# Re-laying a gated attention and FFN block on eight cores: tokens by residue, attention first, a listed order per engine, resident FFN weights

## The chip, the cores and the metric

One Trainium2 chip, eight cores, one sequence of 2048 tokens on each; the cores exchange nothing. The time is that of the slowest core, in microseconds (us) on the device. A program on all eight cores has a second, slower state in some of its executions, in which the cores of one die show a lower granted TensorE clock. Engines: PE is TensorE, PEld its weight loads, DVE VectorE, ACT ScalarE, POOL GpSimd, SP SyncE (it only issues transfers here); a "q" after a name is the engine's sequencer.

## The reference, cut to what matters

```python
h = rms_norm(x, norm_mix_pre)                       # x: 2048 x 1024 per core
u_a, v_a, q, k, v_b, g_a, g_b = split(h @ w_in)     # seven blocks of 1024 columns
y_a = chunked_spatial_gating(gelu(u_a), gelu(v_a))  # branch A: layer norm of v, then tril(W_s) over chunks of 128
y_b = dilated_attention_mixture(q, k, v_b)          # branch B: 16 heads of 64, three patterns below
merged = sigmoid(g_a + b) * (y_a @ w_a_proj) + sigmoid(g_b + b) * (y_b @ w_b_proj)
x = x + rms_norm(merged @ w_out)
f = square(relu(rms_norm(x) @ w_ff1)) @ w_ff2       # 1024 -> 4096 -> 1024
x = x + rms_norm(f)
```

The attention runs every head under (window, dilation) = (128, 1), (512, 4) and (2048, 16), with ALiBi bias, and mixes the three by their softmax denominators. That mixture is the same as adding the three numerators, adding the three denominators, and dividing once.

## The kernel before

Stages run one after the other: norm and transposes, branch A, then attention head pair by head pair, gates, output projection and FFN. The parts that the change touches, with cuts marked:

```python
# operands of a score matmul: tokens in sequence order, so dilations 4 and 16 are steps in the access pattern
def tokapN(T, p, kb, nblk):
    if p == 0: return T[:, 128 * kb:128 * kb + 128 * nblk]
    if p == 1: ...; return T[:, s:s + 4 * (128 * nblk - 1) + 1:4]
    return T[:, kb:SEQ:16]
# Q of each head has 128 rows, of which the other head's 64 are zero:
S.op("dve", lambda e, i=i: e.memset(QZ[i][0][64:128, :], 0.0), ...)
mm(ps[bank][:, ...], tokap(KT[d], slice(0, 128), p, kb), tokapN(QZ[d][hh], p, kb, nblk), ...)
# values: 65 stationary columns (64 of V and one of ones); each dilation is closed in PSUM and added in fp32
mm(ps[bank][:65, acol:acol + n], vaug[d][:, 16 * p + vblk, hh, :], PT[...][:, ptcol:ptcol + n], i == 0, True, ...)
S.op("dve", lambda e: e.tensor_tensor(out=av, in0=ps[bank][0:65, :]..., in1=av, op=ALU.add), ...)
# ... V is transposed on TensorE 48 times per pair; denominators go through DRAM to be inverted and broadcast
S.barrier()                                       # after branch A, after attention, after the gates
for w in range(4):                                # FFN: both weights fetched again for each window
    S.dma("pool", ... out=w1b[b], in_=w1s_d[fq] ...)
    ...
    mm(ps[pk][:, :], w2b[b][:, fb, :], hid[:, fb, :], ...)          # output comes channel-major
    S.op("pe", lambda e, cb=cb: e.transpose(out=..., in_=fT[:, cb, 128 * ti:128 * ti + 128], identity=identf[:]), ...)
```

The softmax here doesn't subtract the row's maximum and nothing guards it: scores larger than these inputs give would overflow.

Of the kernel before, what the change touches and what calls it, by code (L numbers as in the profile page):

```python
# [8 lines left out]
F32 = mybir.dt.float32  # L9
# [6 lines left out]
NCORES = 8  # L16

class Sched:
    ENGS = ("pe", "act", "dve", "pool", "sp")

    def __init__(self, nc):
        self.nc = nc
        self.es = ExitStack()
        self.lists = {e: [] for e in self.ENGS}
        self.sem = {e: self.es.enter_context(nc.semaphore("s_" + e)) for e in self.ENGS}
        self.cnt = {e: 0 for e in self.ENGS}
        self.waited = {e: {} for e in self.ENGS}
        self.lastw = {}
        self.readers = {}
        self.dma_sems = {}  # L30
        self.dma_cnt = {}

    def _need(self, eng, dep):
        key, sem, val = dep
        if key == eng and eng == "pe":
            return
        w = self.waited[eng]
        if w.get(key, 0) >= val:
            return
        w[key] = val  # L40
        self.lists[eng].append(("wait", sem, val))

    def _deps(self, eng, reads, writes):
        for b in list(reads) + list(writes):
            d = self.lastw.get(b)
            if d is not None:
                self._need(eng, d)
        for b in writes:
            for d in self.readers.get(b, ()):
                self._need(eng, d)  # L50

    def _mark(self, tok, reads, writes):
        for b in writes:
            self.lastw[b] = tok
            self.readers[b] = []
        for b in reads:
            self.readers.setdefault(b, []).append(tok)

    def op(self, eng, fn, reads=(), writes=(), signal=True):
        self._deps(eng, reads, writes)  # L60
        if signal:
            self.cnt[eng] += 1
            self.lists[eng].append(("op", fn, self.sem[eng], 1))
            tok = (eng, self.sem[eng], self.cnt[eng])
        else:
            self.lists[eng].append(("op", fn, None, 0))
            tok = (eng, self.sem[eng], self.cnt[eng] + 1)
        self._mark(tok, reads, writes)

    def dma(self, queue, fn, chan, reads=(), writes=()):  # L70
        if chan not in self.dma_sems:
            self.dma_sems[chan] = self.es.enter_context(self.nc.semaphore("d_" + str(chan)))
            self.dma_cnt[chan] = 0
        self._deps(queue, reads, writes)
        self.dma_cnt[chan] += 16
        sem = self.dma_sems[chan]
        self.lists[queue].append(("op", fn, sem, 16))
        tok = ("dma_" + str(chan), sem, self.dma_cnt[chan])
        self._mark(tok, reads, writes)

    def barrier(self):
        toks = [(e, self.sem[e], self.cnt[e]) for e in ("pe", "act", "dve", "pool") if self.cnt[e] > 0]
        toks += [("dma_" + str(c), self.dma_sems[c], self.dma_cnt[c]) for c in self.dma_sems]
        for e in self.ENGS:
            for t in toks:
                if t[0] != e:
                    self._need(e, t)
                elif e != "pe":
                    self._need(e, t)

    def emit(self):
        nc = self.nc
        lists = self.lists

        def replay(lst, e):
            for it in lst:
                if it[0] == "wait":
                    e.wait_ge(it[1], it[2])
                else:
                    ins = it[1](e)  # L100
                    if it[2] is not None:
                        ins.then_inc(it[2], it[3])
# [21 lines left out]
        self.es.close()  # L124

def tokap(T, rows, p, blk):
    if p == 0:
        return T[rows, 128 * blk:128 * blk + 128]
    if p == 1:
        c, n = blk // 4, blk % 4  # L130
        s = 512 * n + c
        return T[rows, s:s + 509:4]
    return T[rows, blk:SEQ:16]

def build_nc():
# [6 lines left out]
    win_d = din("w_in", [56, 128, 1024])  # L142
    wa_d = din("w_a", [8, 128, 1024])
    wb_d = din("w_b", [8, 128, 1024])
    wo_d = din("w_o", [128, 8, 1024])
    w1_d = din("w_1", [128, 8, 4096])
    w2_d = din("w_2", [16, 128, 2048])
    wsT_d = din("wsT", [128, 8, 128])
    bs_d = din("b_s", [1, 1024])
    lgrow_d = din("ln_g_row", [1, 1024])  # L150
    lb_d = din("ln_b", [128, 8])
    bg_d = din("b_gate", [128, 16])
    gains_d = din("gains", [4, 1024])
    ident_d = din("ident", [128, 128], BF16)
    identf_d = din("identf", [128, 128])
    mask_d = din("mask", [128, 128])
    ones_d = din("onesf", [128, 128])
    eb_d = din("eb", [128, 80, 128], BF16)
    out_d = nc.dram_tensor("out", [SEQ, DM], F32, kind="ExternalOutput").ap()
    den_d = nc.dram_tensor("den_scr", [16, SEQ], F32).ap()  # L160
    w1s_d = nc.dram_tensor("w1_bf", [8, 128, 4096], BF16).ap()
    w2s_d = nc.dram_tensor("w2_bf", [8, 128, 4096], BF16).ap()

    S = Sched(nc)
    top = ExitStack()

    def sb(stack, name, shape, dt):
        return stack.enter_context(nc.sbuf_tensor("sb_" + name, list(shape), dt))
# [11 lines left out]
    ssq = stat[:, 0:16]  # L180
    rstd = stat[:, 16:32]
    varall = stat[:, 32:48]
    rstdv = stat[:, 48:64]

    cvn = [0]

# [684 lines left out]
```

## Time and profile before

| what | before |
|---|---|
| time, median of four runs beside the changed kernel | 1584.78 us |
| time, three runs | 1583.41 us |
| PE busy, share of the span | 84% |
| DMA moved per core | 165.70 MB |
| start to first score of attention | about 264 us |
| attention, eight pairs | 492.5 us |
| gates | 225.8 us |
| output projection and FFN | 572.7 us |

The prediction below shows the chain and the stretches. One more reading belongs here, three groups of the page's list of costliest groups (line, engine, operation, operands, shapes, count; busy us, mean ns of one; idle time before them and what ended it):

```profile
L518 ACT ACTIVATE sb_Et<-pst 128x512 bf16<-128x512 f32 x320 | 177.0, 567 | 98.2 <-PE pst L218 40.2
L553 DVE TENSOR_TENSOR sb_acc<-pst,sb_acc 65x512 f32<-65x512 f32 x64 | 69.2, 1081 | 0.1
L557 DVE TENSOR_TENSOR sb_acc<-pst,sb_acc 65x512 f32<-65x512 f32 x64 | 67.0, 1046 | 2.9 <-PE pst L218 0.5
```

The first line is the exponential, 512 columns at a time; the other two are the adds that put dilations 4 and 16 on top of dilation 1. They cost over 1 us each, but VectorE as a whole was not the bound. To compare kernels by stage I use five marks on TensorE's timeline: the first score matmul, the last value matmul, the first gate matmul, the first output projection, the end.

### The profile page before, as it was taken

The page shows a single profiled execution, that of the slowest core. Times are in us where ns is not written, and L with a number is a line of the kernel's source. Part 1 is how long each engine was busy: PE and PEld are TensorE (multiplying, and loading weights), DVE is VectorE, ACT ScalarE, POOL GpSimd, SP SyncE. Part 2 cuts the span into 40 slices and gives each one's busy share as a digit, 9 for nine tenths or more (in the row PEclk, how much of TensorE's full clock was granted, in tenths as well). Part 3 has the DMA queues.
Part 4 walks back from the last instruction along what each step waited for, and adds up shares of the span by engine and source line. Part 5 has one row for each costly group of instructions (what it writes and reads, how often), then busy time and mean ns, then how long its engine had stood idle before and what let it go on. Part 6 is the DMA issues. An engine that isn't in the chain of part 4 may idle for free.

```text
span 1588.4 us, 23161 instructions; the slowest of 8 cores (1567.5 to 1588.4 us)
## 1 busy us (share of the span) xinstructions
PE 1341.3 (84%) x7092; PEld 689.6 (43%) x7092; DVE 663.9 (42%) x1104; ACT 696.4 (44%) x1351; POOL 162.4 (10%) x206
## 2 busy tenths in 40 slices
PE   1498928897998898976199999869999999999994
PEld 1244514554555555543044444324444444444442
DVE  2675661565566555656122332333205404412402
ACT  2423306656756666664055555444314414513302
POOL 1100740001001000000111110000000000000000
PEclk9999959998998989976599999879999999999997
DMA  8830043265465364434574442224245543634532
GB/s 190 154 34 1 1 50 61 42 128 96 107 123 98 100 125 98 103 95 114 80 99 41 41 40 27 94 66 153 113 159 161 184 176 130 199 133 148 197 133 79
DMA packets 116487, 165.70 MB, mean 104 GB/s; under 512 B 79744, under 2 KB 90880, under 8 KB 108160
## 3 DMA queue, kind: packets, MB, share of 16 engines
q0 software_dynamic: 96928, 104.87, 31.8%
q1 hardware_dynamic: 19440, 59.37, 12.0%
q8 instruction: 60, 0.98, 0.2%
q14 instruction: 59, 0.48, 0.1%
HBM read 174.44 MB, written 25.43 MB: 126 GB/s over the span
## 4 chain that ended last, share of the span: by engine, by line
PE 67%; DMA 13%; DVE 8%; issue 5%; ACT 4%; SPq 1%; DVEq 0%; POOL 0%; ACTq 0%; POOLq 0%
PE pst L218 66%; DMA sb_wqkv<-w_in 5%; DMA sb_xt<-x 2%; DMA sb_denbc<-den_scr 2%; DMA sb_dsm<-den_scr 2%; DVE sb_acc L557 2%; DVE sb_bst L311 1%; DVE sb_big L314 1%; DVE sb_t L699 1%; DMA den_scr<-sb_acc 1%; DMA sb_wg<-w_in 1%; PE pst L746 1%; ACT sb_vaug L458 1%; ACT sb_Et L518 1%; ACT sb_gv L308 1%
## 5 line engine op out<-in xcount | busy, mean ns | idle before, releaser
L218 PE MATMUL pst<-sb_h2T,sb_big 128*128 128x512 bf16 x1024 | 228.5, 382 | 2.4 <-ACT sb_h2T L737 1.3
L218 PE MATMUL pst<-sb_hT,sb_w2b 128*128 128x512 bf16 x1024 | 223.6, 379 | 1.5 <-DVE sb_hT L778 1.5
L218 PE MATMUL pst<-sb_hT,sb_wqkv 128*128 128x512 bf16 x768 | 201.6, 412 | 25.2 <-DMA sb_wqkv<-w_in 24.8
L518 ACT ACTIVATE sb_Et<-pst 128x512 bf16<-128x512 f32 x320 | 177.0, 567 | 98.2 <-PE pst L218 40.2
L218 PEld LDWEIGHTS pst<-sb_h2T,sb_big 128*128 128x128 bf16 x1024 | 100.5, 98 | 123.6 <-issue 7.9
L218 PEld LDWEIGHTS pst<-sb_hT,sb_w2b 128*128 128x128 bf16 x1024 | 99.6, 98 | 119.8 <-issue 1.9
L218 PE MATMUL pst<-sb_PT,sb_vaug 128*65 128x128 bf16 (+1 forms) x816 | 112.1, 260 | 44.0 <-DVE sb_PT L534 11.6
L218 PE MATMUL pst<-sb_hT,sb_wg 128*128 128x512 bf16 x512 | 118.2, 385 | 33.5 <-DMA sb_wg<-w_b 33.5
L778 DVE TENSOR_TENSOR sb_hT<-sb_hT 128x512 bf16<-128x512 bf16 x128 | 50.2, 422 | 224.3 <-ACT sb_hT L776 224.1
L218 PEld LDWEIGHTS pst<-sb_hT,sb_wqkv 128*128 128x128 bf16 x768 | 81.1, 107 | 119.3 <-issue 50.5
L528 DVE TENSOR_TENSOR sb_PT<-sb_Et,sb_EBh 128x512 bf16<-128x512 bf16 x176 | 73.4, 425 | 140.4 <-ACT sb_Et L518 136.2
L218 PEld LDWEIGHTS pst<-sb_PT,sb_vaug 128*65 128x65 bf16 x816 | 82.7, 122 | 84.6 <-issue 60.3
L218 PE MATMUL pst<-sb_QZ_1,sb_KT 128*128 128x256 bf16 (+1 forms) x384 | 96.2, 355 | 21.2 <-ACT sb_Et L518 21.1
L776 ACT ACTIVATE sb_hT<-pst 128x512 bf16<-128x512 f32 x128 | 73.0, 595 | 85.2 <-PE pst L218 85.0
L218 PE MATMUL pst<-sb_QZ_0,sb_KT 128*128 128x256 bf16 (+1 forms) x384 | 98.6, 373 | 5.4 <-ACT sb_Et L518 4.1
L792 ACT ACTIVATE sb_yaT<-pst 128x512 f32<-128x512 f32 x32 | 19.1, 597 | 179.7 <-PE pst L218 179.6
L653 ACT ACTIVATE sb_sg<-pst,sb_bg 128x512 f32<-128x512 f32 x64 | 43.4, 678 | 114.2 <-PE pst L218 114.2
L218 PEld LDWEIGHTS pst<-sb_hT,sb_wg 128*128 128x128 bf16 x512 | 50.6, 99 | 95.7 <-issue 36.9
L660 DVE TENSOR_TENSOR sb_tA<-pst,sb_sg 128x512 f32<-128x512 f32 x32 | 22.1, 692 | 114.1 <-ACT sb_sg L656 107.3
L553 DVE TENSOR_TENSOR sb_acc<-pst,sb_acc 65x512 f32<-65x512 f32 x64 | 69.2, 1081 | 0.1
L557 DVE TENSOR_TENSOR sb_acc<-pst,sb_acc 65x512 f32<-65x512 f32 x64 | 67.0, 1046 | 2.9 <-PE pst L218 0.5
L218 PE MATMUL pst<-sb_wout,sb_merged 128*128 128x512 bf16 x256 | 61.1, 395 | 2.2 <-DVE sb_merged L664 2.2
(102 smaller groups left out, 1606.1 us busy)
## 6 DMA issues: line engine op xcount, KB each, us to landing
sb_big<-w_bf POOLq DMA_DIRECT2D x32, 1024.0 KB, 6.3
sb_w2b<-w_bf POOLq DMA_DIRECT2D x32, 1024.0 KB, 5.2
sb_stg<-w POOLq DMA_DIRECT2D x32, 512.0 KB, 5.6
w_bf<-sb_stg SPq DMA_DIRECT2D x32, 512.0 KB, 3.9
sb_xt<-x SPq DMA_DIRECT2D x16, 512.0 KB, 5.3
sb_denbc<-den_scr SPq DMA_DIRECT2D x32, 256.0 KB
sb_xo<-x SPq DMA_DIRECT2D x16, 512.0 KB, 5.3
out<-sb_xo SPq DMA_DIRECT2D x16, 512.0 KB, 2.8
```

The lines of the kernel that those rows point to most:

```text
L218: S.op("pe", lambda e: e.matmul(out, lhsT=lhsT, rhs=rhs, start=start, stop=stop, skip_group_check=True), reads=reads, writes=writes, signa ...
L308: S.op("act", lambda e, hf=hf, pk=pk: e.activation(out=gv[:, 512 * hf:512 * hf + 512], in_=ps[pk + hf][:, :], func=AF.Gelu_apprx_tanh), re ...
L311: S.op("dve", lambda e, hf=hf: e.bn_stats(out=bst[:, 6 * hf:6 * hf + 6], in_=gv[:, 512 * hf:512 * hf + 512]), reads=[f"gv{hf}"], writes=[" ...
L518: S.op("act", lambda e: e.activation(out=Et[es][:, 0:W], in_=ps[bank][:, 0:W], func=AF.Exp), reads=[], writes=[PK[bank], f"Et{es}"])
L528: S.op("dve", lambda e: e.tensor_tensor(out=PT[ptb][:, :].rearrange("p (a q) -> p a q", q=256), in0=Et[es][:, :].rearrange("p (a q) -> p a ...
L553: S.op("dve", lambda e: e.tensor_tensor(out=av, in0=ps[bank][0:65, :].rearrange("p (n i) -> p n i", n=4), in1=av, op=ALU.add), reads=[], w ...
L557: S.op("dve", lambda e: e.tensor_tensor(out=av, in0=ps[bank][0:65, :].rearrange("p (r i) -> p r i", r=4), in1=av, op=ALU.add), reads=[], w ...
L653: S.op("act", lambda e, j=j, cb=cb, po=po: e.activation(out=sg[j][:], in_=ps[po + j][:, :], func=AF.Exp, scale=-1.0, bias=bg[:, 8 * j + cb ...
L660: S.op("dve", lambda e, po=po: e.tensor_tensor(out=tA[:], in0=ps[po + 2][:, :], in1=sg[0][:], op=ALU.mult), reads=["sg0"], writes=[PK[po + ...
L776: S.op("act", lambda e, fb=fb, pk=pk: e.activation(out=hid[:, fb, :], in_=ps[pk][:, :], func=AF.Relu), reads=[], writes=[PK[pk], f"hid{fb}"])
L778: S.op("dve", lambda e, fb=fb: e.tensor_tensor(out=hid[:, fb, :], in0=hid[:, fb, :], in1=hid[:, fb, :], op=ALU.mult), reads=[], writes=[f" ...
L792: S.op("act", lambda e, cb=cb, pk=pk: e.activation(out=fT[:, cb, :], in_=ps[pk][:, :], func=AF.Copy), reads=[], writes=[PK[pk], f"fT{cb}"])
```

## The change: its intent, and the diff

The kernel is written anew. Tokens are stored by residue modulo 16, so that a dilated read is a run of neighbours. Attention comes first, so that branch A's weights arrive behind it. The two heads of a pair use rows 0 to 63 and 64 to 127 of TensorE, and the values of all three dilations add up in one PSUM bank per head. V is made token-major and put into the other two orders by a trip through DRAM. The FFN's weights are converted to bfloat16 in DRAM during attention and loaded once. FFN 2 writes tokens by rows, so that its output needs no transposes. A small scheduler decides the order on each engine beforehand, from assumed durations. The core of it:

```diff
-                    mm(ps[bank][:, ...], tokap(KT[d], slice(0, 128), p, kb), tokapN(QZ[d][hh], p, kb, nblk), ...)
+                rows = slice(64 * hh, 64 * hh + 64)
+                kv, qv = view(KT[d], rows), view(QT[d], rows)
+                ...
+                else:
+                    kk = kv[:, blk, :]
+                    qq = qv[:, blk, :]
+                mms.append((psall[:, sb + hh, n0:n0 + nn], kk, qq, n == 0, n == len(blocks) - 1, nn, False))
-                    S.op("dve", lambda e: e.tensor_tensor(out=av, in0=ps[bank][0:65, :]..., in1=av, op=ALU.add), ...)
+        for j in range(8):            # dilation 1: first matmul of a bank sets, the others add
+            ... mms.append((out(hh, 0, 4, 8 * blk, w), lhs(V0[d], blk, hh), ..., first[hh], False, 4 * w, False))
+        for n2 in range(2):           # dilation 4 adds
+        for a in range(4):            # dilation 16 adds and closes
+            mms.append((ps(bks[hh])[:, 128 * a:128 * a + 128], stg[sd][...], p2t[...], False, a == 3, 128, False))
+    def load_v(hp, prio):             # 32 transfers out of DRAM per head pair, on SyncE's queue
+        ... fns.append(lambda e, ...: e.dma_start(out=V1[d][32 * a:32 * a + 32, 4 * c:4 * c + 4, :], in_=...))
+        ... fns.append(lambda e, b=b: e.dma_start(out=V0[d][:, b, :], in_=s0[b][:, :, 192 * hh:192 * hh + 192]))
+        its.append(... e.dma_start(out=w1s_d[f], in_=w1_d[f]) ...)   # fp32 to bfloat16, DRAM to DRAM, 24 of them
+            P.pe([(ps(bb[hf]), hid[:, fb, 128 * ti:128 * ti + 128], w2[:, fb, 512 * hf:512 * hf + 512], ...)
+                  for fb in range(32)], ...)                         # FFN 2, tokens by rows
+    def dma(self, q, fns, nbytes, chan, ...):
+        o = self._add(q, list(fns), cost, reads, writes, prio, nb=nbytes, chan=chan, lat=2.0, name=name)
```

The last two lines belong to the scheduler: every transfer is taken to land 2 us after its bytes have passed.

## The prediction

> **What bounds the kernel now.** I read the chain that ended last first. It is TensorE for two thirds, transfers for an eighth, and little else:
>
> ```profile
> PE 67%; DMA 13%; DVE 8%; issue 5%; ACT 4%; SPq 1%; DVEq 0%; POOL 0%; ACTq 0%; POOLq 0%
> ```
>
> So I looked for the stages (TensorE's timeline shows where the operands change) and asked for busy time in each stretch. Columns: stretch, its length, busy us and instructions of PE, PEld, DVE, ACT, POOL, then granted clock, DMA share and GB/s.
>
> ```profile
> 0.00:74.50 74.50, 19.76 (x133) 13.74 (x134) 32.23 (x37) 25.72 (x65) 9.98 (x15) 1.00 0.88 180
> 74.50:135.50 61.00, 56.72 (x257) 24.42 (x256) 42.94 (x75) 16.50 (x30) 4.38 (x5) 1.00 0.27 27
> 135.50:212.00 76.50, 64.21 (x385) 32.72 (x383) 47.25 (x58) 23.93 (x40) 40.76 (x31) 0.95 0.00 1
> 212.00:232.70 20.70, 0.02 (x1) 0.06 (x2) 14.36 (x6) 0.00 (x0) 5.69 (x6) 0.50 0.62 78
> 232.70:264.00 31.30, 27.83 (x147) 13.14 (x148) 3.50 (x2) 15.26 (x22) 4.00 (x5) 0.91 0.59 88
> 264.00:756.50 492.50, 419.32 (x2592) 255.19 (x2589) 291.05 (x556) 308.40 (x570) 34.09 (x47) 0.89 0.48 99
> 756.50:789.90 33.40, 0.01 (x1) 0.04 (x2) 4.75 (x5) 0.62 (x2) 4.39 (x5) 0.50 0.58 78
> 789.90:1015.70 225.80, 223.63 (x1025) 100.73 (x1026) 66.65 (x97) 120.97 (x192) 25.34 (x29) 0.99 0.42 46
> 1015.70:1118.00 102.30, 83.06 (x368) 36.71 (x368) 37.57 (x59) 40.53 (x99) 5.30 (x10) 0.87 0.40 144
> 1118.00:1580.00 462.00, 446.75 (x2193) 212.90 (x2192) 123.61 (x214) 144.47 (x334) 28.44 (x54) 0.99 0.42 149
> ```
>
> In order: norm of x and transposes (transfers at 0.88); v of branch A; u and gating; a wait with TensorE empty; the first head pair's projection; attention of eight head pairs; a second empty wait; gates and branch projections; output projection; FFN. The reader is to see two barriers at which TensorE stands still (20.7 and 33.4 us, waiting for weights), one stage filled to 99% (gates), an FFN near that, and attention, 524 us with its lead-in, where TensorE is busy 85% at a granted clock of 0.89.
>
> Busy is not work, so I took paces from the chain and the timeline (start, length, what):
>
> ```profile
> 1150.49 13.81 PE pst L218 x64
> 286.54 1.11 PE L218 MATMUL pst<-sb_QZ_0,sb_KT 128*128 128x128 bf16 x4
> 287.47 0.57 PE L218 MATMUL pst<-sb_PT,sb_vaug 128*65 128x256 bf16 x4
> 292.83 0.41 PE L218 MATMUL pst<-sb_PT,sb_vaug 128*65 128x128 bf16 x4
> 293.07 0.61 PE L454 MATMUL pst<-sb_ident,sb_VT 128*128 128x128 bf16 x8
> ```
>
> Dense matmuls of 512 columns run at 13.81/64 = 0.216 us. Four score matmuls of dilation 16 take 287.47-286.54 = 0.93 us, 0.232 each; four value matmuls of the same 128 columns take 0.24, 0.060 each. The difference is that K and Q are read there with a step of 16 elements. At dilation 4 I read 0.22 us per 256 columns against 0.108 at dilation 1.
>
> **What the Trainium skill says.** "TensorE: Matmul & The Clock Gate", section "Wait — 56ns, not 53.3ns?", gives 215.7 ns from start to start at 512 columns and 55.6 at 128: the trace agrees (0.216; 0.055 to 0.060). Its Part 1 warns of a 13/16 clock with three dense cores on a die: this trace disagrees, all eight cores were granted 0.97 to 0.99 in the FFN. "PSUM — Partial Sum Buffer", "The four PSUM rules", rule 2, says that a matmul without the first flag adds where the bank's bit is set. That is what lets the change sum three dilations in one bank; no run here shows it yet. "TensorEngine Tiling (Array Packing)", "Key Properties", says that row tiles run in parallel but that a change of tiling mode drains TensorE. The new scores use 64-row operands for two heads between full-height matmuls; the trace has none, so I count neither gain nor loss.
>
> **The change, part by part.**
>
> 1. *Dense matmuls.* Their number is the same: 4608 of 512 columns (FFN and output projection 2304, branch A 512, q/k/v 768, gates 1024; V is now made token-major, 256 columns at a time, counted as halves). 4608 x 0.216 = 995 us, a floor that does not move.
>
> 2. *Attention.* Scores have 19,200 columns per head pair before and after, 8.0 us at 2.4 columns per ns. Before, 336 matmuls of dilation 16 pay 0.232-0.060 and 192 of dilation 4 pay 0.22-0.108: 58 + 21 = 79 us, 10 per pair. With tokens sorted by residue these reads are runs, so I drop the 79. The value matmuls become 128 of 64 columns per pair, which I hold at 0.055 (the pace of 128-column loads in the transposes): 7.0 us, plus 3.0 and 1.7 for the other dilations, 11.7 (8 before). The 48 V transposes per pair go (2.7). So a pair with q, k (13.8) and v (6.9) costs 8.0 + 11.7 + 20.7 = 40 us of TensorE. ScalarE: 20 exponentials of up to 1024 columns at 1.02 (the price of a 1024-column ACTIVATE now), 19.5, and 12 log/exp of 512 at 0.6, 7.2: 27 (308/8 = 38 before, as copies leave it). VectorE: masks 14, normalisation 5.5, evictions and reorders of K 10: 30 (36 before; the accumulates, 69.2 + 67.0 us at 1.08 and 1.05 each, go). TensorE stays the bound. Before, waits were (492.5-419)/8 = 9 us per pair; deeper buffers should leave about 5. One bank pair is shared by all four residue classes, and its eviction (two logs, one exp, two products, about 4 us) has 5 us of other matmuls in the new order to hide behind. So six slots at 45, the seventh without v at 38, the last without projections bound by ScalarE at 30: 338 us against 524.
>
> 3. *Start.* 2.6 MB of constants no longer stand ahead of x, and q/k of pair 0 are projected between transposes. The new order puts all 128 v matmuls (14 us) after the last tile. x with first weights is 12 MB; at about 220 GB/s (180 before, at 0.88 and in 256-byte pieces) 54 us, then 17.5 for the rest of the projection: attention begins at about 72, not 232.7, and branch A's 137.5 us move behind it. Both empty waits go (54 us): weights have buffers of their own or are fetched a stage ahead.
>
> 4. *Branch A.* 48 of its 256 v matmuls fill the last pair. The rest: 464 x 0.216 = 100, gating 7, one fp32 product 4; the order starts gating only after five of eight u groups (its operand goes through DRAM), so about 9 us of VectorE eviction stick out: 120 against 137.5.
>
> 5. *Gates.* 1024 x 0.216 = 221; 223 against 225.8. ScalarE's three passes become one tanh, but TensorE was full, so that is worth nothing here.
>
> 6. *Output projection and FFN.* 2304 x 0.216 = 497. The 128 fp32 back-transposes go, as FFN 2 writes tokens by rows; 16 x 8 transposes stay (8). In the new order 184 of the first window's 256 FFN 1 matmuls fill the projection's norm chain. I add 6 for four joints where FFN 2 waits for the last square, 12 for weights that land in space freed by the projection, 10 for the last chain: 533 against 572.7 (1015.7 to 1588.4). That weights stay resident saves some 50 MB of traffic, which was hidden, so no time by itself.
>
> Sum: 72 + 5 (V's first trip through DRAM) + 338 + 120 + 223 + 533 = 1291, so 1290 us. Bare TensorE work, 995 + 64 scores + 94 values + 14 transposes + 11 others, is 1178; with a start of 25 and a tail of 10 nothing can come in below about 1210.
>
> **Rivals.** *DMA binds attention.* V passes through DRAM with 384-byte pieces, 4096 per pair. In the second empty wait 0.58 of 16 engines for 33.4 us, less 77 engine-us for the broadcasts, over 4096 pieces is about 57 ns each; at 65, 16.6 us of all engines per pair. The FFN weight conversion (50 MB read and written) is squeezed from 524 into about 340 us: 12.7 us per pair at the 330 GB/s that busy share and rate of the FFN suggest, and weights, V's store and masks 9 more: 38 of 45 us. "DMA: Bandwidth & Descriptors", Specifications, asks for 512 bytes per piece; the trace's 57 ns supports a fixed cost. Against this rival: V is fetched a slot ahead. If it wins, slots are 52 us and the time about 1340.
>
> *A static order built on too short times.* The scheduler fixes orders beforehand, and its assumed VectorE and ScalarE times are some 10 to 20% below the trace's. In-order TensorE then waits in attention and in the projection chain, where two x buffers give 5 to 6 us per tile: +40 to 60, about 1340.
>
> *Score tiles really overlap.* Two heads at once would take up to 32 us away: 1260.
>
> *The dies throttle.* With hardly any pauses the clock could fall; only the slow state should show that.
>
> **Range.** The errors of slots (8 x 4 us), start (10), joints (20) add to about 45; misses lie more on the high side as the floor is near. 1235 to 1365 should hold it 8 times in 10. Every rival still leaves over 200 us, so faster has 0.97, within 2% 0.02, slower 0.01.
>
> **What would show it.** Right: attention of a pair every 42 to 47 us with TensorE busy above 85% and clock above 0.95, no score group slower than its columns, first scores near 72 us, no empty stretch before the gates, dense paces of 0.216. Wrong: value matmuls of 64 columns well above 0.055, waits for V tiles with DMA share near 1, long TensorE waits for logs or exponentials, an output projection stage over 115 us, or FFN clocks near 0.81 on all dies.

## The result

The changed kernel takes 1352.78 us in the median of four runs (1348.16 to 1375.58, the longest a slow one), against 1584.78 us; the ratio of the fast runs is 0.8538, with a 95% interval of 0.8503 to 0.8574. (A ratio here is the mean time of one kernel's fast runs over that of the other's of the same rounds, so it is not quite the ratio of the medians.) The prediction of 1290 us is 63 us short; its range of 1235 to 1365 holds the result. Outputs are correct.

The chain that ended last, of the changed kernel:

```profile
PE 67%; DMA 13%; SPq 6%; DVE 5%; issue 5%; ACT 3%; DVEq 0%; ACTq 0%; POOL 0%; POOLq 0%
```

TensorE has the same share as before, and so have transfers; new is 6% for SyncE's sequencer, where 1% stood. Next the stretches, with the columns of the prediction's table: up to the first score, attention from its first value matmul on (the 27.6 us between are left out), the rest of branch A, gates, output projection with the first FFN window, FFN:

```profile
0.00:94.40 94.40, 53.16 (x340) 32.85 (x340) 41.74 (x53) 33.65 (x75) 3.51 (x10) 0.89 0.53 137
122.00:448.00 326.00, 273.40 (x3013) 170.50 (x3014) 197.21 (x368) 190.31 (x242) 21.11 (x42) 0.90 0.69 126
448.00:583.00 135.00, 114.02 (x606) 54.98 (x604) 72.89 (x141) 42.29 (x70) 19.45 (x41) 0.92 0.52 121
583.00:804.00 221.00, 221.00 (x1026) 100.18 (x1024) 68.30 (x102) 44.00 (x64) 6.30 (x12) 1.00 0.21 45
804.00:952.00 148.00, 126.03 (x648) 58.72 (x647) 82.45 (x138) 75.48 (x201) 8.87 (x17) 0.93 0.61 211
952.00:1347.00 395.00, 385.18 (x1784) 174.28 (x1782) 85.61 (x176) 85.25 (x192) 0.00 (x0) 0.99 0.11 41
```

The gates are full and the FFN nearly so. Attention is shorter than before by a third, but TensorE is still idle for 53 of these 326 us. TensorE's timeline says where (start, length, operands, count, and in brackets the idle time before and what ended it):

```profile
121.95 0.37 PE L195 MATMUL pst<-sb_PT_0_68,sb_V_0_50 128*128 128x64 bf16 x4 [9.19 <-DMA sb_V_0_50<-v_scr]
168.19 0.37 PE L195 MATMUL pst<-sb_PT_8_76,sb_V_1_51 128*128 128x64 bf16 x4 [6.68 <-DMA sb_V_1_51<-v_scr]
227.97 0.37 PE L195 MATMUL pst<-sb_PT_7_75,sb_V_0_50 128*128 128x64 bf16 x4 [19.98 <-DMA sb_V_0_50<-v_scr]
378.18 0.37 PE L195 MATMUL pst<-sb_PT_3_71,sb_V_0_50 128*128 128x64 bf16 x4 [7.27 <-DMA sb_V_0_50<-v_scr]
546.92 1.86 PE L195 MATMUL pst<-sb_wsT,sb_gc 128*128 128x128 bf16 x16 [15.87 <-DMA sb_gc<-gc_scr]
```

Four times TensorE waits for values coming back from DRAM, 43.1 us in all (the first time just before the stretch begins); the fifth line is the gating operand of branch A, which makes the same trip. A pair with such a wait and one without differ like this (stretches again; the first ends with the 19.98 us wait):

```profile
168.20:228.00 59.80, 38.75 (x418) 24.32 (x419) 28.17 (x53) 25.45 (x32) 2.04 (x4) 0.84 0.77 125
245.20:282.50 37.30, 36.73 (x417) 22.96 (x418) 28.23 (x54) 25.51 (x33) 2.61 (x5) 1.00 0.78 156
```

Undisturbed, a pair takes 37.3 us at full clock, 8 less than I had put on it. Why the values come late is seen in SyncE's timeline and in the list of transfers of attention (first start, length, operands, count; then count, size and median us from issue to landing). The third view is of 138 to 157 us alone, in which the three stores before the longest wait were issued: two queues, GpSimd's and then SyncE's, with packets, MB and share of the sixteen engines (booked where a packet starts, so the sum can pass 100%), and the stores:

```profile
181.58 34.72 SPq L577 DMA_DIRECT2D sb_V_0_52<-v_scr  x16
```

```profile
w_bf<-w POOLq DMA_DIRECT2D x8, 1024.0 KB, 17.7
w_bf<-w POOLq DMA_DIRECT2D x14, 512.0 KB, 9.0
v_scr<-sb_stgV_49 SPq DMA_DIRECT2D x7, 384.0 KB, 11.1
```

```profile
q0 software_dynamic: 201, 2.00, 90.2%
q1 hardware_dynamic: 726, 0.34, 14.6%
v_scr<-sb_stgV_49 SPq DMA_DIRECT2D x3, 384.0 KB, 36.1
```

The sixteen issues of V before the longest wait took SyncE 34.72 us; none of the other fifteen such groups took over 14.8. The stores of V take 11.1 us to land in the median, and the three before that wait took 26.8 to 36.2, beside the conversions of FFN weights (w_bf), while GpSimd's queue alone filled 0.90 of the engines. Whether those conversions are the cause is what the first experiment asks.

### The profile page after: what moved, and what is told of

It reads as the page before. It is cut to its first block, busy times and chain, and to the rows that moved or that the text cites. A ratio compares the mean times of both kernels' runs of the same rounds, so it can differ in the third digit from the quotient of the medians.

```text
span 1346.6 us, 20587 instructions; the slowest of 8 cores (1323.8 to 1346.6 us)
## 1 busy us (share of the span) xinstructions
PE 1191.2 (88%) x7560; PEld 601.9 (45%) x7560; DVE 563.9 (42%) x1007; ACT 483.9 (36%) x857; POOL 59.2 (4%) x122
## 3 DMA queue, kind: packets, MB, share of 16 engines
q8 instruction: 62, 1.02, 0.3%
## 4 chain that ended last, share of the span: by engine, by line
PE 67%; DMA 13%; SPq 6%; DVE 5%; issue 5%; ACT 3%; DVEq 0%; ACTq 0%; POOL 0%; POOLq 0%
PE pst L195 66%; SPq L577 4%; DMA v_scr<-sb_stgV_49 3%; DMA gc_scr<-sb_gct_123 2%; SPq L583 2%; DMA gc_scr<-sb_gct_125 2%; DMA sb_xt_89<-x 2%; DMA sb_xo_148<-x 1%; DVE sb_ybT L705 1%; DMA sb_V_0_50<-v_scr 1%; PE pst L199 1%; DMA sb_gc<-gc_scr 1%; DMA x_scr<-sb_xo_148 1%; DMA v_scr<-sb_stgV_48 1%; DMA sb_w_6_144<-w_bf 1%
## 5 line engine op out<-in xcount | busy, mean ns | idle before, releaser
L195 PE MATMUL pst<-sb_w_146,sb_hid 128*128 128x512 bf16 x1024 | 221.7, 379 | 2.7 <-issue 1.4
L195 PEld LDWEIGHTS pst<-sb_w_146,sb_hid 128*128 128x128 bf16 x1024 | 100.0, 98 | 124.0 <-issue 3.7
L968 ACT ACTIVATE sb_hid<-pst 128x512 bf16<-128x512 f32 x128 | 76.4, 597 | 136.5 <-PE pst L195 135.9
L969 DVE TENSOR_TENSOR sb_hid<-sb_hid 128x512 bf16<-128x512 bf16 x128 | 54.2, 424 | 144.8 <-ACT sb_hid L968 142.1
L629 ACT ACTIVATE sb_Et_82<-pst 128x1024 bf16<-128x1024 f32 (+1 forms) x54 | 52.0, 962 | 65.7 <-PE pst L195 59.0
L195 PE MATMUL pst<-sb_hT,sb_wqk_62 128*128 128x512 bf16 x256 | 67.0, 412 | 4.9 <-ACT sb_hT L496 2.7
L629 ACT ACTIVATE sb_Et_84<-pst 128x1024 bf16<-128x1024 f32 (+1 forms) x53 | 51.2, 965 | 39.4 <-PE pst L195 33.6
L195 PE MATMUL pst<-sb_wva,sb_hT 128*128 128x512 bf16 x256 | 59.8, 393 | 5.5 <-ACT sb_gv_121 L782 4.7
L195 PE MATMUL pst<-sb_hT,sb_wqk_63 128*128 128x512 bf16 x256 | 62.9, 391 | 0.4 <-DVE sb_stgV_49 L561 0.2
L629 ACT ACTIVATE sb_Et_83<-pst 128x1024 bf16<-128x1024 f32 (+1 forms) x53 | 51.8, 977 | 24.9 <-PE pst L195 18.9
L195 PE MATMUL pst<-sb_hT,sb_wg_129 128*128 128x512 bf16 x256 | 57.9, 379 | 0.0
L195 PE MATMUL pst<-sb_hT,sb_wg_130 128*128 128x512 bf16 x256 | 57.9, 379 | 0.0
L195 PEld LDWEIGHTS pst<-sb_wout,sb_merged 128*128 128x128 bf16 x256 | 25.1, 100 | 39.9 <-issue 13.9
L195 PEld LDWEIGHTS pst<-sb_wva,sb_hT 128*128 128x128 bf16 x256 | 25.3, 101 | 38.1 <-issue 11.7
L195 PEld LDWEIGHTS pst<-sb_hT,sb_wqk_62 128*128 128x128 bf16 x256 | 24.6, 104 | 38.9 <-issue 18.8
L195 PEld LDWEIGHTS pst<-sb_hT,sb_wg_130 128*128 128x128 bf16 x256 | 25.0, 98 | 30.2
L195 PEld LDWEIGHTS pst<-sb_hT,sb_wg_129 128*128 128x128 bf16 x256 | 25.0, 98 | 30.0
L195 PEld LDWEIGHTS pst<-sb_hT,sb_wqk_63 128*128 128x128 bf16 x256 | 23.6, 100 | 29.9 <-issue 7.1
```

What stands on the lines that cost most here:

```text
L195: e.matmul(out, lhsT=l, rhs=r, start=st, stop=sp, skip_group_check=True))
L629: P.act(lambda e: e.activation(out=et[:, :, 0:W], in_=psall[:, sb:sb + 2, 0:W], func=AF.Exp, scale=0.125), 2 * W, [], [et.key()], [sb, sb ...
L968: P.act(lambda e, fb=fb, bk=bk: e.activation(out=hid[:, fb, :], in_=ps(bk), func=AF.Relu), 512, [], [hid.key(fb)], [bk])
L969: P.dve(lambda e, fb=fb: e.tensor_tensor(out=hid[:, fb, :], in0=hid[:, fb, :], in1=hid[:, fb, :], op=ALU.mult), 512, [hid.key(fb)], [hid.k ...
```

## The experiments

The stages of the profiled core, by the five marks (us; "A and gates" is from the last value matmul to the first output projection, "F" from there to the end). In two of the runs, weights reloaded and conversions in the gates, the profiled core had a lower clock in attention than others of the same run, of which more below:

| kernel | first score | attention | A and gates | F | span |
|---|---|---|---|---|---|
| changed kernel | 94.4 | 353.3 | 355.8 | 543.0 | 1346.6 |
| no conversions | 96.1 | 310.8 | 350.4 | 573.6 | 1330.8 |
| values of pair 0 early | 89.3 | 363.6 | 357.1 | 543.8 | 1353.8 |
| weights reloaded | 95.0 | 363.6 | 352.1 | 567.2 | 1377.8 |
| conversions in the gates | 94.5 | 332.3 | 372.2 | 584.5 | 1383.5 |
| conversions in the gates, values of pair 0 early | 87.9 | 310.0 | 372.2 | 593.7 | 1363.8 |
| plan told of slow gating trip | 93.1 | 360.2 | 354.1 | 547.2 | 1354.6 |
| no conversions, same rows | 95.4 | 331.5 | 350.7 | 569.6 | 1347.2 |
| candidate | 89.1 | 309.2 | 350.8 | 540.3 | 1289.4 |

### Conversions cut to slivers (e1_noconv)

```diff
-    e.dma_start(out=w1s_d[f], in_=w1_d[f])
+    e.dma_start(out=w1s_d[f][0:16, 0:64], in_=w1_d[f][0:16, 0:64])      # w2 likewise; same order, no traffic
-    load_w1: in_=w1s_d[f]
+    load_w1: in_=w1_d[f]                                                # cast on load, so the result stays right
```

> The 24 weight conversions through DRAM shrink to slivers and FFN weights are cast when they are loaded; the order of every engine is unchanged and the result stays right. Theory T (traffic: the conversions, 50 MB, slow V's trip through DRAM and the gating operand's): TensorE's waits for V at pairs 2, 3 and 6 (6.7, 20.0, 7.3 us) fall below 2 us each, the store of V lands in about 7 us instead of 27, the wait of 15.9 us for the gating operand falls below 8, so attention and branch A lose 35 to 50 us; the output projection gets 5 to 20 us longer as the loads read twice the bytes. Net 20 to 40 us faster than the changed kernel, about 1315. Theory S (the 32 issues of V per pair, 18.7 us on SyncE, make V late whatever the traffic): the waits stay within 3 us of what they are, net below 10 us.

Measured: 1330.73 us (1329.69 to 1332.39), ratio 0.8382 (0.8347 to 0.8416), correct. The same two views of this kernel, SyncE's timeline and the transfers of attention:

```profile
159.64 8.34 SPq L577 DMA_DIRECT2D sb_V<-v_scr  x16
```

```profile
v_scr<-sb_stgV SPq DMA_DIRECT2D x11, 384.0 KB, 2.7
```

The same sixteen issues take 8.34 us instead of 34.72, and V's stores land in 2.7 us in the median instead of 11.1. The waits for V fall to one of 8.2 us, that of pair 0, and attention from 353.3 to 310.8 us. The waits are 35 of these 42.5 us; the rest is a slower pace after each wait (groups of four 64-column matmuls stand 0.21 us apart just after the 19.98 us, 0.117 later). All eight cores show it: 26 to 43 us of waits for V in the changed kernel, 7.6 to 8.4 here. So the conversions made the other three waits, though they stand in GpSimd's queue and V's in SyncE's. The Trainium skill says so in general ("DMA: Bandwidth & Descriptors", section "Issuing engines are not separate DMA queues": transfers of all engines end on the same sixteen and interleave); this pair of runs agrees and gives the price, though it does not tell the sixteen engines from DRAM itself, which both kinds of transfer used as well. Two things did not follow the expectation. The wait for the gating operand stayed, 14.78 us, so it is not made by conversions. And the output projection and FFN took 31 us more, with TensorE waiting 25.5 us for tiles of x: weights cast on load are read as fp32 there, twice the bytes, which is how I read it, and most of the gain went back.

### Values of pair 0 window by window (e3_vearly)

```diff
-    proj_qk(0, lambda i, n: -1990.0 + 20 * i)
-    proj_v(0, range(8), lambda i: -1980.0 + 20 * i)
+    for w in range(4):
+        proj_qk(0, lambda i, n: -1990.0 + 20 * i, range(w, w + 1))
+        proj_v(0, range(2 * w, 2 * w + 2), lambda i: -1980.0 + 20 * i)
```

> For pair 0 the v projection is recorded window by window between the q/k projections, so that the two PSUM banks do not force it behind all of them. Theory B (the banks' recorded order, not late weights, pushed the 128 v matmuls behind the last x tile): V's stores leave by about 80 us, first value matmul at 100 to 108 instead of 121.9, whole kernel 12 to 22 us faster. Rival (the start is bound by the x tiles and the in-order engines, v only moves the wait): less than 6 us.

Measured: 1353.94 us (fast runs 1344.44 to 1355.37), ratio 0.8492 (0.8432 to 0.8553), correct. The first score comes 5 us sooner, the first value matmul at 116.40 us (121.95 in the changed kernel), later than expected and with a wait of 8.81 us still before it. Over the whole kernel the waits for V are 43.0 us, as before. The time gained at the start was lost again in attention, which was 10 us longer; some 7 us of that is idle time of TensorE for which the profile names no releaser, and its cause is open. No gain is shown.

### Both heads' scores on the same rows (e4_samerows)

```diff
-                rows = slice(64 * hh, 64 * hh + 64)
+                rows = slice(0, 64)
```

> Scores of both heads are taken from partitions 0 to 63 (the result is wrong on purpose). Theory O (two heads in different row halves of the array overlap, which halves the scores): the pace of scores of 256 columns goes from 0.068 to about 0.108 us, of 128 columns from 0.030 to about 0.056, an undisturbed pair from 37.2 to 40.5 to 41.5 us, the kernel 20 to 32 us slower, about 1375. Rival (the pace comes from something else, as shorter weight loads of 64 rows): no change of pace or time.

Measured once: 1355.23 us. The pace changed as it should: eight score matmuls of 256 columns take 0.97 us from start to start of the next work (0.121 each), where the changed kernel takes 0.54 (0.068 each). So two heads on different rows do run beside each other. Yet the time hardly moved: in this run the waits for V were 27.1 us and not 43.1. The extra work fell into time that TensorE would have waited. This run cannot price the overlap, so I repeated it without the waits, next.

### The same without conversions (e10_noconv_samerows)

> Result wrong on purpose. Two edits: the conversions cut to slivers, as in the run that measured 1330.7 us (ratio 0.838), and both heads' scores taken from rows 0 to 63, so that they can't run beside each other. With the waits for V out of the way, theory M (the earlier run with the same rows on the unchanged traffic hid its cost in those waits): TensorE's busy time on scores rises by about 33 us (64.8 and 29.8 us where it was 41 and 20), and now the attention grows by 25 to 35 us: 1355 to 1368 us, ratio 0.854 to 0.862. Rival (the scores lie beside ScalarE's exponentials, TensorE is not what bounds an undisturbed pair): under 10 us, ratio below 0.845.

Measured: 1351.28 us (fast runs 1348.72 to 1351.59), ratio 0.8521 (0.8501 to 0.8540), against 0.8382 without conversions alone. The score groups of the run without conversions, then of this one (count; busy us, mean ns; idle before):

```profile
L195 PE MATMUL pst<-sb_QT,sb_KT 64*128 64x256 bf16 x432 | 40.8, 277 | 8.6 <-ACT sb_Et L629 8.6
L195 PE MATMUL pst<-sb_QT,sb_KT 64*128 64x128 bf16 x336 | 19.9, 217 | 4.4 <-ACT sb_Et L629 4.4
```

```profile
L195 PE MATMUL pst<-sb_QT,sb_KT 64*128 64x256 bf16 x432 | 64.1, 274 | 6.2 <-ACT sb_Et L629 6.2
L195 PE MATMUL pst<-sb_QT,sb_KT 64*128 64x128 bf16 x336 | 29.7, 221 | 3.6 <-ACT sb_Et L629 3.6
```

The mean duration of one matmul does not tell the difference at all (277 against 274 ns), as the matmuls overlap in time; the busy time of the group does: 33 us more. Attention grows from 310.8 to 331.5 us, so 21 of the 33 reach the time. That is less than the 25 to 35 I expected and more than the rival's 10. The overlap of two heads is a gain of about 20 us in this kernel, once the waits are gone.

### A step in Q (e5_qstride) and a step in K (e6_kstride)

```diff
-                    qq = qv[:, blk, :]
+                    qq = QT[d][rows, blk:2048:16]     # e5: moving operand; e6: kk = KT[d][rows, blk:2048:16], stationary
```

> Scores of dilation 16 read Q with a step of 16 elements again, K in runs (the result is wrong on purpose). Theory M (the moving operand's step made 0.232 us of 0.056 before): the 256 matmuls of 128 columns go from 0.030 to at least 0.11 us each (0.232 over two overlapping rows), 20 to 50 us slower in all. Rival (the step in K's weight load did it): no change beyond 5 us.

> Result wrong on purpose. Scores of dilation 16 with the stationary operand K read at a step of 16 elements instead of contiguous; its twin with the moving operand Q at that step measured 1.02 us for eight matmuls of 128 columns, where the changed kernel takes 0.24. Theory Q (only the moving operand's step is dear): the eight take 0.24 to 0.35 us, the group's mean of 217 to 224 ns for the 128-column scores stays under 260 ns. Rival K (a strided stationary operand is loaded as slowly): 0.5 us or more for the eight, mean above 300 ns.

Measured once each: 1359.52 and 1354.86 us. The groups of 128-column scores in the run with stepped Q, then with stepped K:

```profile
L195 PE MATMUL pst<-sb_QT,sb_KT 64*128 64x128 bf16 x336 | 42.3, 360 | 4.3 <-ACT sb_Et L629 4.3
```

```profile
L195 PE MATMUL pst<-sb_QT,sb_KT 64*128 64x128 bf16 x336 | 22.3, 233 | 4.3 <-ACT sb_Et L629 4.3
```

In the changed kernel the six groups of this form sum to 22.0 us. A step of 16 elements in the moving operand Q adds 20 us (eight matmuls in 0.91 to 1.02 us, up to 0.127 each, where the changed kernel takes 0.030); the same step in the stationary operand K adds next to nothing (0.3 us of busy time; eight matmuls mostly take 0.30 to 0.40 us, in the changed kernel 0.23 to 0.33). So at dilation 16 what the residue order is worth in scores lies in Q; the step of dilation 4 was not tried alone. The Trainium skill speaks of it in "SBUF — State Buffer", in "Door 1: The DMA port swizzle" (a note on 16-byte lines: a step is free as long as two accesses fall in one line, eight elements of bfloat16). A step of 16 is outside that and is dear here, so the runs agree; but the kernel before paid 0.22 us instead of 0.108 already at a step of 4 (in Q and K), which the note would have free. As with the scores above, the whole time hardly shows the 20 us, because the waits for V were there to take it in (34.1 us left in the run with stepped Q).

### FFN weights loaded again for each window (e7_reload)

```diff
+        if w < 3:
+            for f in range(8):
+                load_w1(f, L0 + 100 * w + 34 + f)
+            ...                                        # and the sixteen blocks of the second weight
```

> One part undone: the FFN weights stay resident in the changed kernel; here both are loaded again from the bfloat16 copies for each of the four token windows (24 more megabytes a core), the order on TensorE unchanged. Theory R (residency is worth nothing in time, because the FFN stage is bound by TensorE's dense pace at 0.216 us a matmul and its transfers lie beside it): the FFN stage stays within 3 us of 386.7 us, all of it at joints between windows, ratio to before 0.852 to 0.858, and the DMA share of the stage goes from 0.11 to about 0.2-0.25. Rival (residency saves waits): the first matmuls of windows 1 to 3 wait for their weights, over 5 us each, and the time rises by 15 us or more.

Measured: 1381.95 us (fast runs 1375.09 to 1382.69), ratio 0.8703 (0.8660 to 0.8745), correct. Neither side was right in full. From the first FFN 2 matmul to the end the run takes 401.5 us against 394.8, 7 us more, all at joints (on all eight cores 401.2 to 401.6 against 394.7 to 394.8); within a window the pace stays at 0.216 and the DMA share goes from 0.11 to 0.40, more than the 0.2 to 0.25 expected. That part of theory R holds nearly. But the time rose by 29 us over the changed kernel's. Seventeen of them lie in the output projection: the scheduler put the reload for the second window ahead of blocks that the first still needed, and TensorE waited 16.0 us for w_bf where it had waited 4.8. (The order on TensorE was not kept, as I had written it would be; at the three joints after the first it now waits 1.4 to 3.2 us, where two of them had no wait.) Attention was 10 us longer too, with nothing changed in it; the profiled core 5 was granted a clock of 0.84 there, and core 4 0.86, where the other six had 0.90 or 0.91. So residency is worth 7 us in the windows as such, and more where a reload shares the first window's fetch.

### Conversions moved into the gates (e_convgates, e8_both)

```diff
-            for _ in range((nconv * (4 * hp + c + 1)) // 32 - (nconv - len(conv))):   # in attention
-                P.prio = b0 + 25 * c + 10
-                conv.pop(0)()
+            if it >= 1 and conv:                                                      # in the gates
+                conv.pop(0)()
-        if 2 <= cb < 4: load_w1(cb - 2, ...)     # the first two blocks of weights are loaded later, too
+        if 4 <= cb < 6: load_w1(cb - 4, ...)
```

> The 24 conversions of FFN weights move from attention to the stage of the gates, where the DMA engines were busy only 0.21; nothing else is changed, and the result stays right. Theory T (the waits for V are made by the conversion traffic): the waits for V go from 43 us to about 8 (only pair 0's, as in the run whose conversions were cut to slivers), attention is shorter by 30-40 us with the half clock after the waits gone, ratio to before 0.830 to 0.840, that is 1315 to 1332 us; the gates stay at 221 to 225 us, and the out-projection may wait some us more for the late FFN weights. Rival (the gain of the cut conversions came in part from less traffic overall): the gates or F0 grow by 15 us or more and the ratio stays above 0.845.

> The conversions in the stage of the gates, and the values of pair 0 recorded window by window. With V's transfers fast, the early values should now show: theory B expects the first value matmul at 108 to 117 us and the wait for V of pair 0 gone or under 5 us, 5 to 10 us below the run with the conversions moved alone (about 1310 to 1322 us, ratio 0.825 to 0.835). Rival (SyncE's 32 issues of V and the x tiles set the start whatever TensorE's order): within 4 us of it.

Measured: conversions moved, 1385.16 us (fast runs 1385.03 and 1385.29), ratio 0.8737 (0.8679 to 0.8795); with the early values of pair 0 as well, 1363.91 us (1359.60 to 1376.66), ratio 0.8616 (0.8555 to 0.8676). Both are correct, and both are slower than the changed kernel, the first clearly; of the second no fast run is below 1359.60 us where the changed kernel's end at 1355.56, but the intervals of the ratios still touch. The waits for V did go as theory T said, to one of 8.4 and one of 10.0 us, and in the second run attention is down by 43 us. All of it was given back later. The waits of TensorE in the first of these runs, and the transfers of its output projection stage:

```profile
PE pst L195 <- DMA sb_gc<-gc_scr: 29.1, 1, 29.1
PE pst L195 <- DVE sb_xo L925: 27.6, 5, 11.5
```

```profile
w_bf<-w POOLq DMA_DIRECT2D x6, 512.0 KB, 19.5
```

Six conversions ran in the output projection. The kernel fills GpSimd's queue in a fixed order, and the later fetches of gate weights in it wait 24 to 26 us each for TensorE; behind each the scheduler, which took a conversion for 7 to 14 us of all bandwidth, had let only two pass. Output projection and FFN then took 584.5 and 593.7 us instead of 543.0. The wait for the gating operand doubled to 29 us as well: with the conversions gone from the plan, the scheduler expected that operand sooner and put 72 u matmuls ahead of it where 136 had stood. The gates themselves stayed at 221 us. In the first of the two runs attention was 332.3 us on the slowest core, core 1, 22 more than in the second. Core 1, then core 2 of the same run, with the columns of the stretches:

```profile
122.00:240.00 118.00, 117.79 (x1174) 71.94 (x1171) 75.96 (x140) 70.61 (x89) 2.15 (x4) 0.82 0.46 87
122.00:240.00 118.00, 116.36 (x1293) 72.12 (x1290) 86.97 (x163) 79.69 (x101) 2.69 (x5) 0.99 0.47 100
```

Cores 0, 1, 4 and 5 were granted 0.81 to 0.82 here, with TensorE hardly idle, and took 329 to 333 us for attention; the other four had 0.98 or 0.99 and took 309 to 312. So half of each die was slowed in a run that counts as fast. Cores 4 and 5 show the same in the run with the weights reloaded and in the candidate's first run below; what brings it on is open. The loss does not hang on it: the four cores with the full clock are at 1355 to 1364 us, where the changed kernel's eight are at 1324 to 1347.

### The plan told that the gating trip is slow (e9_gclat)

```diff
-    P.dma("sp", ... out=gscr_d[n], in_=t_[:] ...)                  # both transfers, lat=2.0 by default
+    P.dma("sp", ... out=gscr_d[n], in_=t_[:] ...).lat = 8.0
```

> Only the plan is told that each of the two DMAs of the gating operand takes 8 us to land where it had assumed 2; the instructions are the same ones, in another order: eleven and a half more groups of u matmuls (92 matmuls, 20 us) stand ahead of the first gating matmul. Theory O (the 15.87 us wait is made by the static order, built on too short a DMA time, not by lack of work): the wait falls below 4 us, branch A from 134 to 118-122 us, the time by 12-15 us: 1337 to 1342 us, ratio 0.844 to 0.848. Rival L (the wait is the last link of a chain whose end is fixed later by the mask-and-gate work on VectorE behind it): the wait shrinks, but the gates start at the same time within 4 us and the ratio stays above 0.850.

Measured: 1353.30 us (fast runs 1348.04 to 1356.15), ratio 0.8505 (0.8449 to 0.8562), correct. Two of TensorE's waits:

```profile
PE pst L195 <- DMA sb_gc<-gc_scr: 8.8, 1, 8.8
PE pst L195 <- DVE sb_tmpm L836: 5.4, 7, 1.8
```

The wait fell from 15.87 to 8.8 us, and the gates started 119.4 us after attention instead of 134.8, as theory O said. But 5.4 us of waiting for VectorE came in, and part of the matmuls of branch A now lie among the gates: the two stages together take 354.1 us against 355.8. This is the slowest core. On six of the eight the wait fell below 4 us (11.8 to 15.9 in the changed kernel), and the median of the two stages over all cores went from 352.3 to 345.9 us. So theory O has the wait right and about half of its gain in these stages, and the rival, whose ratio just holds, is wrong about the start of the gates. In time the run is not told apart from the changed kernel (intervals overlap).

### A candidate from the findings (e11_best, e12_best_again)

```diff
-        for f in range(8):          # conversions of the first weight
+        for f in (2, 4, 5, 6, 7):   # blocks 0, 1 and 3 are cast on load, in the gates
-            ... 3e6, f"cv{f % 2}", ...           # size told to the scheduler
+            ... 1.2e6, f"cv{f % 2}", ...         # second weight: 0.6e6 and channels 2 and 3 of their own
+            if it >= 1 and conv: conv.pop(0)()   # in the gates, none in attention
-    xo = [buf(f"xo{i}", (176 + 4 * i) * K, [1024], F32) for i in range(2)]
+    xo = [buf(f"xo{i}", o * K, [1024], F32) for i, o in enumerate((176, 180, 112, 116))]
+    ...                             # and the edits of e3_vearly and e9_gclat
```

> A correct candidate that puts the findings together. Twenty-one conversions in the stage of the gates, told to the plan as short, so that four are issued per column block from its start and the last are through before the out-projection (in the earlier run of this kind the last six ran into it); three of the eight blocks of the first FFN weight cast on load; values of pair 0 recorded window by window; the plan told of 8 us for the DMAs of the gating operand; four buffers for x in the out-projection. Theory: waits for V only pair 0's (8-10 us), wait for the gating operand under 10 us, out-projection stage at most 125 us: 1290 to 1310 us, ratio 0.815 to 0.828. Rival (traffic moved is traffic given back: the queue of the weights is one FIFO and the gates can't take it): a wait of over 10 us appears in the gates, or the out-projection stage stays above 140 us, and the time stays above 1325 us, ratio over 0.835.

> The same kernel as the candidate before, on another chip if it falls so: there three of its four runs were slow or had single cores at a lower clock (core 4 at 0.949 and 1311.5 us where core 0 took 1278.4), and no ratio came out. Theory: in fast runs 1285 to 1312 us, ratio to before 0.815 to 0.828. Rival (the single cores at 1311 are the kernel's own state, in which one core's attention loses clock): the fast runs lie at 1308 to 1315 us, ratio 0.825 to 0.832.

The first time, three of its four runs were slow (1312.59 us in the median; 1291.52 in the fast one). Cores 4 and 5 of the profiled run, at 0.82 from 122 to 240 us, needed some 22 us more for attention than the other six. Again with five rounds, it takes 1292.87 us (fast runs 1290.88 to 1293.35), ratio 0.8149 (0.8136 to 0.8161), correct: faster than both kernels, and the rival's 1308 to 1315 us did not come. The wait for V is 8.4 us and that for the gating operand 4.3, as expected. The stretches, cut at the five marks:

```profile
89.10:398.30 309.20, 281.48 (x3162) 174.28 (x3162) 212.66 (x399) 202.79 (x256) 9.81 (x20) 0.96 0.46 91
398.30:519.90 121.60, 111.95 (x584) 53.60 (x582) 65.22 (x126) 42.74 (x70) 18.23 (x39) 0.97 0.58 125
519.90:749.10 229.20, 224.52 (x1052) 101.71 (x1050) 75.53 (x115) 43.97 (x64) 16.98 (x34) 0.99 0.68 102
```

The DMA share of attention is 0.46 where it was 0.69, and that of the gates 0.68 where it was 0.21: the conversions now lie under the stage that TensorE fills. Of the 57.2 us between the two profiled spans, 44.1 come from attention, 5.3 from the start, 5.0 from branch A and gates, 2.7 from the output projection and FFN. Which of the candidate's edits to the queue kept the conversions out of the output projection was not taken apart.

## Why the prediction was right, and where it was not

The profiled span is 1346.6 us and my sum was 1291. The steps differ like this: start 94.4 for 72 (+22); attention with V's first trip 353.3 for 343 (+10); branch A and gates 355.8 for 343 (+13); output projection and FFN 543.0 for 533 (+10). They add to the 55. All four are on the same side, and that the range held owes something to luck, as attention shows.

1. *Dense matmuls.* Right. 32 dense matmuls stand 6.91 us apart in the FFN, 0.216 each; the gates took 221 us and the FFN ran at a granted clock of 0.99.

2. *Attention.* The sum came out nearly right from two terms that were wrong in opposite directions. The slots of 45 us were too long: undisturbed pairs take 37.3. I had counted no gain from two heads on separate rows (0.068 us per 256 columns and head, where columns alone would ask 0.107), and had held the 64-column value matmuls at 0.055; groups of four stand 0.117 us apart, 0.029 each. That is 3 us less for each of the two, and the 5 us per slot left for waits were hardly used there. Against that I had 5 us for V's first trip and nothing for the later ones, and 43.1 us of waiting came. Freed of conversions the same attention takes 310.8 us, of which 8.2 are a wait: the work is 302.6 us and not 338. The step that failed is the overlap. I had the mechanism on the page, as the rival "DMA binds attention", and argued it away with "V is fetched a slot ahead". The profile shows why that did not hold at the longest wait: stores that land 27 to 36 us after their issue, and then 16 issues that take 35 us, eat more than a slot of 37. So 35 us less work, 38 more waits and 7 to 8 of slower pace after them make the +10. (The 79 us of strided reads that I dropped were too many: 336 are all scores of 128 columns, and 256 of them are of dilation 16, which gives about 65. They are not in the sum, which goes by columns.)

3. *Start.* The largest miss. I divided 12 MB by 220 GB/s. The stretch shows 137 GB/s over 94.4 us at a DMA share of 0.53, so the transfers were not the bound that I had assumed; TensorE stood idle for 41 us in it, mostly for normalised x tiles that came one at a time. That both removed barriers and branch A's weights left the path was right. Recording v early gave 5 us (first score at 89.3); what sets the other 17 was not tested and stays open.

4. *Branch A.* The term was too small by 15 us, by one wait: the gating operand, 15.87 us. I had named the order and its operand's trip through DRAM, and put 9 us of VectorE's work on it, but no time on the trip. Cutting the traffic left the wait in place (14.78 us). Ordering more matmuls ahead of it about halved it on the slowest core and all but ended it on six others; VectorE's chain then took over some of the time, so part of my 9 us is real.

5. *Gates.* Right: 221.0 us for 223.

6. *Output projection and FFN.* Nearly right in the sum. Two of the four joints wait 1.4 us, as I had put them, the other two not at all; late weights cost 4.8 us and not 12. What I had not put in the sum are waits for tiles of x (8.4 us) and for the norm chain (5.9), and a clock of 0.93 in the projection stage. "Residency saves no time by itself" was too strong: undone, the windows take 7 us more, and the fetches collide in the first.

Of the rivals, DMA in attention came true in its cost, but not by the averages that I had worked out: over attention the engines were busy 0.69, and they were full in the stretch that mattered (0.90 by GpSimd's queue alone from 138 to 157 us). (A slip in it: 149 GB/s at a share of 0.42 suggest 355 GB/s and not 330; it changes little.) Overlapping score tiles came true too; the two nearly cancel. The static order built on short times is seen in branch A. Throttling was seen on whole dies only in slow runs, and on half dies, for a part of attention, in three profiled runs, two of which count as fast. Of my signs, 42 to 47 us a pair and a clock above 0.95 in attention did not come (37.3 or 59.8 us; 0.90), and one of the wrong side did: the output projection stage, to its last transpose, took about 122 us.

## What to carry to other kernels

When a chain of transfers feeds TensorE a stage ahead, ask what else is in flight then: background traffic on another engine's queue made these stores four times slower. Put it under a stage that computes without fetching, but check that a queue in order does not push it further than you meant. And price a saving only where nothing else waits: work added or taken away beside a 43 us wait does not show in the time.

## What the Trainium skill lacked or had wrong

- "SBUF — State Buffer", the note on 16-byte lines: a step of up to eight bfloat16 elements is called free. The kernel before paid 0.22 us per 256 columns at a step of 4 against 0.108. No page says that the cost falls on the moving operand alone; a step of 16 in 256 of the 128-column scores made them 20 us dearer in Q and 0.3 us dearer in K.
- "TensorE: Matmul & The Clock Gate", Part 1, has all-core kernels run at a 13/16 clock. All eight cores had 0.97 to 0.98 over the whole span in fast runs of the candidate; only in slow runs one die had 0.81 to 0.82 over the span.
- The same Part 1 has its limiter take the whole die. In one fast run cores 0, 1, 4 and 5 were granted 0.81 to 0.82 for 118 us, near the 13/16 that it names, while the other two cores of each die had 0.98 or 0.99.
- "TensorEngine Tiling (Array Packing)": gives "Up to 2×" for a dimension of 64, as theory, and no measured pace for two row tiles of 64. Here it is 0.068 us per matmul of 256 columns against 0.121 on the same rows. The drain at a change of tiling mode that it warns of is small here: an undisturbed pair, which switches many times, took 37.3 us, where its matmuls at their paces sum to 34.7 (13.8 for q and k, 7.4 for v, 4.9 for scores, 8.6 for values). With the 0.9 us by which the scores lie above half the time of their columns, all switches and everything else cost 3.5 us a pair at most (an estimate).
- "DMA: Bandwidth & Descriptors" says that all issuing engines share the sixteen DMA engines, but not at what price: with conversions from DRAM to DRAM in flight, stores of 384 KB took 11.1 us in the median, and 36.2 at most, instead of 2.7, and one group of sixteen issues on SyncE 34.72 us instead of 8.34 (the other groups 7.6 to 14.8).
